# A hybrid gMLP / SSD block on one core: scan steps metered by engine weights, residual tiles fetched one tile ahead, last norms moved behind the first feed-forward unit

## The chip, the cores and the metric

The kernel runs on 1 of the 8 cores of one Trainium2 chip. The metric is the device time of one execution in microseconds. Everything below is read from the kernel's code, from the order of its built program, from three timed runs and from one profiled execution.

## What is computed

One layer of a hybrid backbone over 2048 latent tokens of width 1024, and 256 context tokens that only supply starting states. All matrices are float32.

```python
hl  = rms(x) * norm1_w * (1 + sc1) + sh1
proj = hl @ w_in                      # u, v (gMLP), z, x/B/C, dt
xbc = silu(conv5(xbc) + b)            # centred depthwise convolution
y   = ssd(forward) + flip(ssd(flipped))      # 16 heads, chunks of 128, states of 128 x 64
g   = (y + xs * d_skip) * silu(z);  ssd_out = rms(g, per group) * ssd_norm_w
gm_out = gelu(u) * (W_s @ rms(gelu(v)) * gm_norm_w + gm_bs)
x   = x + g1 * (concat(gm_out, ssd_out) @ w_out)
hl  = rms(x) * norm2_w * (1 + sc2) + sh2
x   = x + g2 * ((silu(hl @ w1) * (hl @ w3)) @ w2)
out = rms(x) * final_norm_w
```

## The kernel before

Every large product is made of three TensorE products of a high and a low part (`mm3`, lines 220 to 232): one output tile of 128 x 512 takes 24 matmuls of 512 columns, summed in one PSUM bank (tag `mmp`, four banks; the small products use four banks of tag `smp`). ScalarE makes the high part of each weight unit and VectorE the low part (line 217).

The tokens go in two blocks of 1024, and block 1 is projected first. The change concerns the long stretch that begins when block 0 projects z. Its main line is a chain of generators, one `yield` for each output tile of 24 matmuls: 16 tiles of `proj_z`, 16 of `proj_v`, 16 of `proj_u`, then `out_half` three times, 16 tiles each: block 1 with the gMLP half of w_out, block 0 with the gMLP half, block 0 with the SSD half. In the text these stages are z, v, u, oA, oB, oC. `early` loads the inputs of the next stage some tiles ahead (`load_mix`). The fourth `out_half` (block 1, SSD half; oD) comes after it, beside `border`, which prepares the first feed-forward unit. Then follow `ffn1(0)`, `ffn2(0)`, `ffn1(1)`, `ffn2(1)`; the feed-forward products use a seven-product scheme, whose moving operands `hl` 1 to 7 are made from the normed x (`prep_hl`, lines 997 to 1038) and in part parked in DRAM (`cscr`) and fetched back (`hl_back`, line 1044).

Beside the main line runs the side line: the last eight chunks of the backward state scan (`ssd_bwd`, 16 steps), then `ssd_y` for 16 chunks and two groups. One iteration of `ssd_y` (a chunk and a group) has two `y_seg` steps, which build the masked decay matrices out of 128 x 128 pieces (lines 722 to 733: two DMAs that spread a row of `fscr`, ScalarE line 728, VectorE line 729, ScalarE line 730, VectorE line 731, four times each, an exponential, a product on POOL), and `y_out` in three parts: the products with the two states and the diagonal product (lines 750 to 757), the state update and the sums (761 to 767), the gate with z read back from `zscr` (770 to 772). A chunk is normed by `y_norm` (a Newton square root of 11 small VectorE instructions, then line 780 on ScalarE), and `y_store` transposes it on TensorE (line 787) and stores it (line 790). The records of a chunk (`rec_sb`) lie in two buffers, the working tiles `tma` in 14.

`run` (line 876) sets the order: after each main step it takes `SIDE` = 2.74 side steps, whatever main or side step it is. The built program keeps an order near that one on each engine.

In `out_half` a tile's residual (x, or the x written by the half before) is loaded by line 849 after the tile's matmuls are issued, line 850 on VectorE adds the scaled product, and line 851 stores the sum. All of these transfers, the weights and the scan's loads among them, are issued in order by one queue, SP. In the second half the squares of the sums are gathered (`sq_acc`), and `rstd_store` (line 263) turns them into the reciprocal root of the next norm: a matmul with ones, a logarithm and an exponential on ScalarE, three VectorE steps, a store to `r2scr`. For block 1 the first 512 tokens' is made inside oD, the second's in the first unit of `ffn1(0)`.

Of the kernel before, what the change touches and what calls it, by code (L numbers as in the profile page):

```python
# [14 lines left out]
P = 128  # L15
# [14 lines left out]
NT2B = 3  # L30
# [7 lines left out]
SIDE = 2.74  # L38
# [44 lines left out]
def kernel(ctx: ExitStack, tc: tile.TileContext, xT, ctxp, cc, crow, wad1, wad2, vecs, rows,  # L83
# [506 lines left out]
    def proj_u(blk, hs):  # L590
        for h0 in range(0, 8, 2):
            us = [unit(U_U + h0), unit(U_U + h0 + 1)]
            for j in range(2):
                ts_ = slice((blk * 2 + j) * TB, (blk * 2 + j + 1) * TB)
                for i, (hi, lo) in enumerate(us):
                    m = tmp()
                    DMA.dma_start(m[:, :TB], mscr[h0 + i][:, ts_])
                    ps = mmp()
                    mm3(ps, [(hi[:, k * P:(k + 1) * P], lo[:, k * P:(k + 1) * P], hs[j][k][:, 0, :], hs[j][k][:, 1, :]) for k in range(KT)])
                    t = gelu2(ps, tmp)  # L600
                    V.tensor_tensor(out=t[:, :TB], in0=t[:, :TB], in1=m[:, :TB], op=ALU.mult)
                    DMA.dma_start(gmscr[h0 + i][:, ts_], t[:, :TB])
                    yield

    def proj_v(blk, hs):
# [17 lines left out]
        for hh in range(2):  # L623
            us = [unit(U_V + hh * 4 + i) for i in range(4)]
            for j in range(2):
                vh = []
                for c in range(4):
# [14 lines left out]
                    yield  # L642
                prev = (hh, j, vh)
        mixing(*prev)
        yield

    def proj_z(blk, hs):
        for g in range(2):
            us = [unit(U_Z + g * 4 + i) for i in range(4)]
            for c in range(8):  # L650
# [6 lines left out]
                yield  # L657
# [42 lines left out]
    def ssd_bwd(rp, hp, chunks):  # L700
        for c in chunks:
            for g in range(2):
                DMA.dma_start(hscr[c][:, g * TB:(g + 1) * TB], hst[(1, g)])
                if c > 0:
                    rc = load_rec(rp, c, g, False)
                    hst[(1, g)] = state_step(hp, rc, g, c, 1, hst[(1, g)])
                yield
# [7 lines left out]
    def y_seg(st, c, g):  # L715
        rc = st["rc"]
        Gt = []
        for q in range(2):
# [16 lines left out]
            yield  # L735
# [8 lines left out]
        yield  # L744

    def y_out(st, c, g, ms):
# [11 lines left out]
        yield  # L758
# [9 lines left out]
        yield  # L768
# [4 lines left out]
        yield  # L773
        return ya

    def y_norm(ys, ms):
# [4 lines left out]
        yield  # L781

    def y_store(ys, c):
        for g in range(2):
# [7 lines left out]
            yield  # L792
# [44 lines left out]
    def out_half(blk, half, hs, tmp=tma, last=None, last_acc=None):  # L837
        acc = [None, None]
        pend = None
        for m0 in range(0, 8, 2):  # L840
            us = [unit(U_O + half * 8 + m0), unit(U_O + half * 8 + m0 + 1)]
            for j in range(2):
                ts_ = slice((blk * 2 + j) * TB, (blk * 2 + j + 1) * TB)
                for i, (hi, lo) in enumerate(us):
# [3 lines left out]
                    t = tmp()  # L848
                    DMA.dma_start(t[:, :TB], xT[m * P:(m + 1) * P, ts_] if half == 0 else x2scr[m][:, ts_])
# [5 lines left out]
                    if half == 1:  # L855
                        acc[j] = sq_acc(acc[j], t[:, :TB], last_acc if last_acc and j == 1 and m == 0 else tmp)
# [8 lines left out]
                    yield  # L865

    def early(gen, total, lead, fn, box):
        for i in range(total):
            if i == total - lead:
                box.extend(fn())  # L870
            if next(gen, 0) is StopIteration:
                break
            yield
        yield from gen
# [70 lines left out]
    for _ in xbc(0, hs, None, dt_block(0, stat(hs))):  # L945
        pass
    m1, m0, s0, s1, h2 = [], [], [], [], []
    run((chain(proj_z(0, hs), proj_v(0, hs), early(proj_u(0, hs), 16, 6, lambda: [load_mix(2, 0), load_mix(3, 0)], m1),
               early(out_half(1, 0, m1), 16, 4, lambda: [load_mix(0, 0), load_mix(1, 0)], m0),
               early(out_half(0, 0, m0), 16, 4, lambda: [load_mix(0, 1), load_mix(1, 1)], s0),  # L950
               early(out_half(0, 1, s0), 16, 2, lambda: [load_mix(2, 1), load_mix(3, 1)], s1)), 1),
        (chain(ssd_bwd(rp, hp, range(7, -1, -1)), ssd_y(rp)), SIDE))


# [5 lines left out]
    accp = ctx.enter_context(tc.tile_pool(name="accp", bufs=1, reuse_waits="tile"))  # L960
# [148 lines left out]
    def ffn1(blk, raws, first=None):  # L1109
# [45 lines left out]
        for t in range(NJ + 1):  # L1155
# [10 lines left out]
            if blk == 0 and t == 0:  # L1166
                rstd_store(*box.pop())
# [200 lines left out]
```

## Time and profile before

| | us |
|---|---|
| median of 3 runs | 3001.41 (2999.85 to 3001.45) |
| the profiled execution, its own time | 3001.86 |
| its span | 2999.7 |
| PE busy | 2827.3 (94%) |
| weight loads busy | 2253.5 (75%) |
| VectorE (DVE) busy | 2002.9 (67%) |
| ScalarE (ACT) busy | 1295.7 (43%) |
| GpSimd (POOL) busy | 633.1 (21%) |

2.2 us of the execution lie outside the span. The busy time of PE is that of matmuls whose ends are modelled. Where PE has been idle for some microseconds, the granted clock falls to half for a while, which shows in the matmuls that follow: a busy PE is then a slower one. A number in brackets behind a row is the idle time of the engine before it, and what ended it.

### The profile page before, as it was taken

Reading aid. Unit: us, or ns where it says so; the run is one execution under the profiler, and the core shown is the slowest. Engines: PE = TensorE matmul, PEld = TensorE weight load, DVE = VectorE, ACT = ScalarE, POOL = GpSimd, SP = SyncE. Lnnn points to the kernel's source line nnn. Section 1 sums busy time; section 2 is a strip of 40 time slices with the busy share of each in tenths; the row PEclk is TensorE's granted clock in tenths of the full one; section 3 lists DMA queues with packets and bytes.
Section 4 is the critical chain, followed back from the end, with each engine's and each line's share of the span. In section 5 each row is a group of like instructions: output and inputs, shape, how many; then the busy total and the mean of one; then the engine's idle time right before and its main releaser. Section 6 shows DMA issues by size and latency. Waiting matters only on the chain. (4 is left out here: it accounts for less than half of the span.)

```text
span 2999.7 us, 37193 instructions
## 1 busy us (share of the span) xinstructions
PE 2827.3 (94%) x12474; PEld 2253.5 (75%) x12474; DVE 2002.9 (67%) x3412; ACT 1295.7 (43%) x2387; POOL 633.1 (21%) x550
## 2 busy tenths in 40 slices
PE   7999999999998988999888799999999899999997
PEld 2788778878676767777767588888778788888885
DVE  6777966886788889778764555555776544445555
ACT  4444343344355556445452533333554333333443
POOL 3100000210131223222202244444110322221000
PEclk8999999999999999999999899999999999999998
DMA  5222567732754668877756544445766433224664
GB/s 222 88 91 88 186 217 231 261 120 82 231 168 148 194 203 254 242 244 235 210 163 221 172 158 159 160 158 165 256 224 206 142 106 106 96 100 131 226 193 157
DMA packets 295531, 525.94 MB, mean 175 GB/s; under 512 B 28838, under 2 KB 89638, under 8 KB 295340
## 3 DMA queue, kind: packets, MB, share of 16 engines
q1 hardware_dynamic: 295340, 523.57, 54.4%
q8 instruction: 98, 1.61, 0.2%
q14 instruction: 93, 0.76, 0.1%
HBM read 380.84 MB, written 142.62 MB: 175 GB/s over the span
## 5 line engine op out<-in xcount | busy, mean ns | idle before, releaser
L979 DVE TENSOR_TENSOR hl<-w,hl 128x1024 fp32r<-128x1024 f32 x286 | 371.9, 1306 | 308.9 <-ACT hl L978 127.1
L978 ACT CAST hl<-w 128x1024 fp32r<-128x1024 f32 x286 | 298.3, 1049 | 427.4 <-PE mmp L1094 121.5
L230 PE MATMUL mmp<-actt,whi 128*128 128x512 f32 x1120 | 458.2, 409 | 14.4 <-DVE t L850 8.0
L231 PE MATMUL mmp<-actt,whi 128*128 128x512 f32 x1120 | 448.5, 400 | 0.0
L232 PE MATMUL mmp<-actt,wlo 128*128 128x512 f32 x1120 | 445.8, 398 | 0.0
L1093 PE MATMUL mmp<-hl,hl 128*128 128x512 f32 x704 | 276.2, 392 | 5.5 <-DVE t L1201 2.3
L1095 PE MATMUL mmp<-hl,hl 128*128 128x512 f32 x704 | 276.0, 392 | 0.5 <-DVE hl L979 0.5
L1094 PE MATMUL mmp<-hl,hl 128*128 128x512 f32 x704 | 275.8, 392 | 0.0
L230 PEld LDWEIGHTS mmp<-actt,whi 128*128 128x128 f32 x1120 | 216.4, 193 | 65.9 <-DVE t L850 10.5
L231 PEld LDWEIGHTS mmp<-actt,whi 128*128 128x128 f32 x1120 | 216.4, 193 | 48.5 <-issue 5.5
L232 PEld LDWEIGHTS mmp<-actt,wlo 128*128 128x128 f32 x1120 | 215.6, 193 | 47.8 <-issue 1.7
L1093 PE MATMUL smp<-hl,hl 128*128 128x512 f32 x528 | 210.1, 398 | 16.5 <-ACT hl L978 16.5
L230 PE MATMUL mmp<-whi,actt 128*128 128x512 f32 x512 | 211.8, 414 | 0.0
L1094 PE MATMUL smp<-hl,hl 128*128 128x512 f32 x528 | 208.9, 396 | 0.0
L1095 PE MATMUL smp<-hl,hl 128*128 128x512 f32 x528 | 207.4, 393 | 0.0
L232 PE MATMUL mmp<-whi,actt 128*128 128x512 f32 x512 | 207.2, 405 | 0.0
L231 PE MATMUL mmp<-wlo,actt 128*128 128x512 f32 x512 | 205.8, 402 | 0.0
L985 DVE TENSOR_TENSOR t<-smp,t 128x512 f32<-128x512 f32 x88 | 60.5, 688 | 187.8 <-PE smp L1095 146.5
L1093 PEld LDWEIGHTS mmp<-hl,hl 128*128 128x128 f32 x704 | 132.4, 188 | 36.1 <-issue 2.7
L452 DVE SCALAR_TENSOR_TENSOR tma<-xin,cw,tma 128x512 f32<-128x512 f32 x192 | 144.3, 751 | 21.5 <-ACT tma L450 15.9
L985 POOL TENSOR_TENSOR w<-w 128x512 f32<-128x512 f32 x44 | 58.6, 1333 | 458.5 <-DVE hl L979 316.9
L733 POOL TENSOR_TENSOR tma<-tma 128x512 f32<-128x512 f32 x64 | 87.4, 1366 | 318.9 <-ACT tma L732 222.4
(267 smaller groups left out, 5875.7 us busy)
## 6 DMA issues: line engine op xcount, KB each, us to landing
w<-in_wall_dram SPq DMA_DIRECT2D x110, 512.0 KB, 4.1
ws<-in_wall_dram SPq DMA_DIRECT2D x104, 512.0 KB, 4.4
ascr<-t SPq DMA_DIRECT2D x154, 256.0 KB, 4.0
w<-ascr SPq DMA_DIRECT2D x154, 256.0 KB, 2.8
tma<-fscr SPq DMA_DIRECT2D x128, 256.0 KB, 5.8
w<-wscr SPq DMA_DIRECT2D x88, 256.0 KB, 3.5
t<-x2scr SPq DMA_DIRECT2D x74, 256.0 KB, 4.6
w<-in_wall_dram SPq DMA_DIRECT2D x66, 256.0 KB, 3.6
```

The lines of the kernel that those rows point to most:

```text
L230: PE.matmul(ps, lhsT=lh, rhs=rh, start=(i == 0), stop=False)
L231: PE.matmul(ps, lhsT=lh, rhs=rl, start=False, stop=False)
L232: PE.matmul(ps, lhsT=ll, rhs=rh, start=False, stop=(i == n - 1))
L452: V.scalar_tensor_tensor(out=acc[:, :n], in0=raw[:, j:j + n], scalar=cw[:, ch, j:j + 1], in1=acc[:, :n], op0=ALU.mult, op1=ALU.add)
L733: G.tensor_tensor(out=A, in0=A, in1=fb, op=ALU.mult)
L978: S.copy(hi, x)
L979: eng.tensor_tensor(out=lo, in0=x, in1=hi.bitcast(F32), op=ALU.subtract)
L985: eng.tensor_tensor(out=o, in0=a, in1=b, op=ALU.add)
L1093: PE.matmul(ps, lhsT=hi[:, ms_], rhs=t[:, 0, :], start=first and k == 0, stop=False, skip_group_check=not first)
L1094: PE.matmul(ps, lhsT=hi[:, ms_], rhs=t[:, 1, :], start=False, stop=False, skip_group_check=not first)
L1095: PE.matmul(ps, lhsT=lo[:, ms_], rhs=t[:, 0, :], start=False, stop=k == 3, skip_group_check=not first)
```

## The change

Three edits.

The meter. `run` with `SIDE` gives way to `paced`. Each main and side step now yields a pair of weights, TensorE and VectorE microseconds (`W_MM` with `W_Z`, `W_V`, `W_U`, `W_O` for a main tile, `W_MIX` for the loading of a stage's inputs, and `W_ST` to `W_TR` for the side steps). After a main step, side steps are taken while the VectorE sum is below `SHARE` = 1.15 times the TensorE sum. A side step that needs a gate tile not yet written waits for it (`zdone`), and a stage that reads the stored scan makes sure it is there (`need`, `stored`).

The residual. `out_half` loads the residual of the next tile ahead of the sum of this one (`fetch`).

The norms. Both of block 1's `rstd_store` are made after the second round (t = 1) of the first feed-forward unit. For that a second buffer of the sum of squares is needed, and the pool `t2b` shrinks from three tiles to two: one more of the x tiles of `ffn2` is taken from the 14 tiles of `t2`.

```diff
-NT2B = 3
+NT2B = 2
-SIDE = 2.74
+SHARE = 1.15
+W_MM = 5.4
+W_Z, W_V, W_U, W_O, W_MIX = 1.4, 5.8, 2.8, 1.45, 11.4
+W_ST, W_SEG, W_Y1, W_Y2, W_Y3, W_NORM, W_TR = (0.85, 2.1), (0, 3.2), (2.9, 1.4), (0.85, 3.0), (0, 0.7), (0, 3.7), (1.0, 0)
...
@@ y_out
-        yield
+        yield W_Y2
+        while zdone[0] < min(g * 8 + c + 1, g * 8 + 8):
+            yield None
         zt = tma()[:, :TB]
...
@@ out_half
+        def fetch(m, j):
+            t = tmp()
+            ts_ = slice((blk * 2 + j) * TB, (blk * 2 + j + 1) * TB)
+            DMA.dma_start(t[:, :TB], xT[m * P:(m + 1) * P, ts_] if half == 0 else x2scr[m][:, ts_])
+            nxt.append(t)
+        todo = [(m0 + i, j) for m0 in range(0, 8, 2) for j in range(2) for i in range(2)]
+        fetch(*todo.pop(0))
...
-                    t = tmp()
-                    DMA.dma_start(t[:, :TB], xT[m * P:(m + 1) * P, ts_] if half == 0 else x2scr[m][:, ts_])
+                    t = nxt.pop(0)
+                    if todo:
+                        fetch(*todo.pop(0))
...
                             pend = (acc[j], r2scr[blk * 2 + j], tmp)
-                            if j == 1:
-                                if last is None:
-                                    rstd_store(*pend)
-                                else:
-                                    last.append(pend)
+                            if last is not None:
+                                last.append(pend)
                                 pend = None
-                    yield
+                            elif j == 1:
+                                rstd_store(*pend)
+                                pend = None
+                    yield W_MM, W_O
-    def early(gen, total, lead, fn, box):
-        for i in range(total):
+    def early(gen, total, lead, fn, box, need=0):
+        for i, w in enumerate(gen):
             if i == total - lead:
+                yield need
                 box.extend(fn())
-            if next(gen, 0) is StopIteration:
-                break
-            yield
-        yield from gen
+                yield (0, W_MIX)
+            yield w
+    def paced(main, side, share):
+        pe = dve = 0.0
+        for w in main:
+            if isinstance(w, int):
+                while stored[0] < w:
+                    next(side)
+                continue
+            pe, dve = pe + w[0], dve + w[1]
+            while dve < share * pe:
+                w = next(side, None)
+                if w is None:
+                    break
+                pe, dve = pe + w[0], dve + w[1]
+        for _ in side:
+            pass
...
@@ ffn1
-            if blk == 0 and t == 0:
-                rstd_store(*box.pop())
+            if box and t == 1:
+                for b in box:
+                    rstd_store(*b)
+                box.clear()
```

What the meter does to VectorE's queue in stage v is seen here, at two of the 16 tiles. Before (575 and 577 are the gelu of a v tile, 635 to 243 its square root, 637 its scaling, 729 and 731 the scan's 128 x 128 steps, 757 and 763 the scan's outputs):

```order
L637 TENSOR_TENSOR xin<-xin,sml 128x512
L731 SCALAR_TENSOR_TENSOR tma<-rec_sb,dt_sb,tma 128x128 x4
L577 SCALAR_TENSOR_TENSOR xin<-xin,mmp 128x512
L777 TENSOR_SCALAR sml<-sml 128x2
L217 TENSOR_TENSOR wlo<-ws,whi 128x1024
L729 SCALAR_TENSOR_TENSOR tma<-tma,acs 128x128 x4
L757 TENSOR_TENSOR tma<-smp,eac 128x512
L635 TENSOR_SCALAR sml<-sml 128x4
L575 SCALAR_TENSOR_TENSOR xin<-xin,mmp 128x512
L238 TENSOR_SCALAR sml<-sml 128x4
L763 TENSOR_TENSOR h_2515<-h_2515,smp 128x512
```

Now (lines are 3 higher up to line 640):

```order
L580 SCALAR_TENSOR_TENSOR xin<-xin,mmp 128x512
L640 TENSOR_TENSOR xin<-xin,sml 128x512
L220 TENSOR_TENSOR wlo<-ws,whi 128x1024
L638 TENSOR_SCALAR sml<-sml 128x4
L241 TENSOR_SCALAR sml<-sml 128x4
L242 TENSOR_SCALAR sml<-sml 128x4
L244 TENSOR_TENSOR sml<-sml 128x4
L578 SCALAR_TENSOR_TENSOR xin<-xin,mmp 128x512
L245 SCALAR_TENSOR_TENSOR sml<-sml 128x4
```

Most of the scan's rows have left stage v. Counted by the matmul of line 751 in TensorE's order, the iterations that stand in z, v, u, oA, oB, oC were 3, 5, 7, 6, 6, 5 and are 5, 2, 5, 9, 8, 3; the chunks transposed in oA, oB, oC were 4, 3, 3 and are 4, 4, 3.

SP's queue at the end of oD, before (849 loads a residual, 851 stores a sum, 1044 fetches `hl` 6 and 5 back, 267 stores a norm):

```order
L849 DMA t2_14390<-x2scr7_168 128x512
L1199 DMA x2t_17959<-x2scr0_161 128x512
L851 DMA x2scr7_168<-t2_14390 128x512
L1044 DMA t2_14401<-cscr6_0_191 128x512
L849 DMA t2_14434<-x2scr6_167 128x512
L1054 DMA w4_14608<-in_wall_dram 128x1024
L851 DMA x2scr6_167<-t2_14434 128x512
L849 DMA t2_14476<-x2scr7_168 128x512
L267 DMA r2scr2_159<-t2_14440 1x512
L851 DMA x2scr7_168<-t2_14476 128x512
L1044 DMA t2_14522<-cscr5_0_195 128x512
```

Now (856 loads, 873 stores, 1080 fetches back):

```order
L856 DMA t2_14356<-x2scr7_168 128x512
L873 DMA x2scr6_167<-t2_14318 128x512
L856 DMA t2_14392<-x2scr6_167 128x512
L873 DMA x2scr7_168<-t2_14356 128x512
L1080 DMA t2_14403<-cscr6_0_191 128x512
L856 DMA t2_14436<-x2scr7_168 128x512
L873 DMA x2scr6_167<-t2_14392 128x512
L1237 DMA x2t_17959<-x2scr0_161 128x512
L873 DMA x2scr7_168<-t2_14436 128x512
L1080 DMA t2_14512<-cscr5_0_195 128x512
```

Each residual's load now stands ahead of the store of the tile before it; it stood behind. The norm's store is gone from here.

ScalarE's queue where the first of block 1's norms is made, before (between the casts of `hl` 6, line 978, at the end of oD; 248 and 249 are the logarithm and the exponential):

```order
L978 CAST hl_0_14495<-t_14401 128x512
L248 ACT_TABLE_LOAD
L248 ACTIVATE t_14440<-smp,eps_t 128x512
L978 CAST hl_1_14496<-t_14403 128x512
L249 ACT_TABLE_LOAD
L249 ACTIVATE t_14440<-t_14440 128x512
L978 CAST hl_2_14497<-t_14405 128x512
```

Now (1169 is a silu of the first unit, 251 and 252 the same two functions, 1014 the cast):

```order
L1169 ACTIVATE t_14804<-t_14804 128x512
L251 ACT_TABLE_LOAD
L251 ACTIVATE t_14822<-smp,eps_t 128x512
L252 ACT_TABLE_LOAD
L252 ACTIVATE t_14822<-t_14822 128x512
L1014 CAST hl_14717<-t_14706 128x512
```

Four instructions that stood between the casts of the border stand behind a silu of the first unit.

## Rows read from the trace of the kernel before

**Rows 1.** Busy time by stage: z, v, u, oA, oB, oC, oD, border.
```profile
core 0: us, PE busy (x) PEld busy (x) DVE busy (x) ACT busy (x) POOL busy (x), PEclk, DMA share, GB/s
735.40:860.20 124.80, 120.81 (x509) 89.72 (x509) 89.48 (x174) 50.99 (x120) 22.16 (x18) 0.99 0.60 193
860.20:1006.10 145.90, 127.79 (x591) 101.87 (x590) 128.33 (x379) 86.47 (x278) 33.32 (x28) 0.94 0.47 145
1006.10:1149.80 143.70, 132.06 (x610) 101.86 (x609) 117.98 (x277) 79.11 (x196) 41.12 (x31) 0.96 0.72 228
1149.80:1287.20 137.40, 124.81 (x549) 97.88 (x548) 113.50 (x242) 71.31 (x171) 38.60 (x31) 0.94 0.81 244
1287.20:1416.00 128.80, 121.36 (x538) 94.81 (x537) 96.51 (x210) 61.85 (x151) 35.58 (x30) 0.96 0.76 231
1416.00:1549.40 133.40, 117.97 (x522) 92.92 (x521) 93.21 (x190) 64.00 (x138) 21.19 (x19) 0.94 0.65 200
1549.40:1656.70 107.30, 96.80 (x388) 76.25 (x386) 51.77 (x75) 38.43 (x56) 17.05 (x11) 0.94 0.62 201
1656.70:1697.40 40.70, 20.10 (x65) 13.14 (x64) 29.11 (x37) 24.18 (x35) 7.47 (x5) 0.75 0.68 232
```

**Rows 2.** Whom PE waited for, 735.4 to 1549.4: total, times, longest.
```profile
PE smp L787 <- ACT tma L780: 34.5, 9, 8.4
PE smp L615 <- DVE xin L637: 6.0, 2, 4.6
```

**Rows 3.** Whom VectorE waited for, the same stretch.
```profile
DVE tma L729 <- ACT tma L728: 56.7, 38, 4.4
...
DVE tma L850 <- DMA tma<-in_xT_dram: 11.7, 5, 4.2
...
DVE tma L850 <- DMA tma<-x2scr: 10.8, 7, 6.2
```

**Rows 4.** Timeline of PE in oC, with its longest wait.
```profile
1506.19 1.12 PE L787 MATMUL smp<-ident,tma 128*128 128x128 f32 x4 [8.45 <-ACT tma L780]
...
1507.53 0.63 PE L231 MATMUL mmp<-actt,whi 128*128 128x512 f32 x1
...
1512.85 0.39 PE L230 MATMUL mmp<-actt,whi 128*128 128x512 f32 x1
...
1515.35 1.02 PE L750 MATMUL smp<-h,rec_sb 128*128 128x512 f32 x2
...
1518.77 0.48 PE L230 MATMUL mmp<-actt,whi 128*128 128x512 f32 x1
```

**Rows 5.** Timeline of the queue SP shortly before that wait.
```profile
1478.59 0.53 SPq L849 DMA_DIRECT2D tma<-x2scr  x1
1489.10 0.32 SPq L851 DMA_DIRECT2D x2scr<-tma  x1
```

**Rows 6.** Whom the queue SP waited for, oA to oC.
```profile
SPq L851 <- DVE tma L850: 64.5, 33, 5.6
SPq L851 <- DMA tma<-x2scr: 34.3, 10, 7.2
SPq L687 <- POOL tma L766: 27.7, 11, 3.4
```

**Rows 7.** Whom PE and VectorE waited for, oD and border.
```profile
PE mmp L230 <- DVE t L850: 8.0, 6, 3.0
...
DVE t L850 <- DMA t<-x2scr: 26.2, 9, 4.4
```

**Rows 8.** Timelines of ACT, SP and PE in the border.
```profile
1666.37 1.28 ACT L248 ACT_TABLE_LOAD   x1
...
1674.77 0.42 SPq L849 DMA_DIRECT2D t<-x2scr  x1
...
1679.52 9.87 SPq L1044 DMA_DIRECT2D t<-cscr  x16
...
1683.11 0.79 PE L1093 MATMUL smp<-hl,hl 128*128 128x512 f32 x1 [16.53 <-ACT hl L978]
```

**Rows 9.** Whom PE waited for in the first `ffn2`, 2090 to 2400.
```profile
PE mmp L1221 <- DVE hl L979: 4.5, 2, 2.4
```

More of the change, by code (lines that the diff above doesn't have):

```diff
@@ L641, in proj_v @@
                         mixing(*prev)
-                    yield
+                    yield W_MM, W_V
                 prev = (hh, j, vh)
         mixing(*prev)
-        yield
+        yield 0, 0
+    zdone = [0]
     def proj_z(blk, hs):
@@ L656, in proj_z @@
                 DMA.dma_start(zscr[blk * 8 + c][:, g * TB:(g + 1) * TB], t[:, :TB])
-                yield
+                zdone[0] += 1 - blk
+                yield W_MM, W_Z
     def state_in(rc, g, ci, d):
@@ L734, in y_seg @@
             Gt.append(A)
-            yield
+            yield W_SEG
         st["G"] = Gt
@@ L743, in y_seg @@
         st["hb"] = hb
-        yield
+        yield 0, 0
     def y_out(st, c, g, ms):
@@ L772, in y_out @@
         S.activation(zt, ya, AF.Square, accum_out=ms[:, g:g + 1])
-        yield
+        yield W_Y3
         return ya
@@ L780, in y_norm @@
             S.activation(ys[g], ys[g], AF.Copy, scale=r[:, g:g + 1])
-        yield
+        yield W_NORM
     def y_store(ys, c):
@@ L791, in y_store @@
                           t.rearrange("p (i t) -> p i t", t=P))
-            yield
+            yield W_TR
+        stored[0] = c + 1
+    stored = [0]
     def ssd_y(rp):
@@ L855, in out_half @@
                     if half == 1:
[L856 removed]
+                        acc[j] = sq_acc(acc[j], t[:, :TB], last_acc if last_acc and m == 0 else tmp)
                         if m == 7:
                             pend = (acc[j], r2scr[blk * 2 + j], tmp)
[L859 to L868 removed]
+                            if last is not None:
+                                last.append(pend)
+                                pend = None
+                            elif j == 1:
[4 more added lines that the diff above has]
+        for i, w in enumerate(gen):
             if i == total - lead:
+                yield need
                 box.extend(fn())
[L871 to L874 removed]
+                yield (0, W_MIX)
[15 more added lines that the diff above has]
+            pass
     def run(*gens):
@@ L947 @@
     m1, m0, s0, s1, h2 = [], [], [], [], []
[L948 to L952, printed above, removed]
+    paced(chain(proj_z(0, hs), proj_v(0, hs), early(proj_u(0, hs), 16, 6, lambda: [load_mix(2, 0), load_mix(3, 0)], m1),
+                early(out_half(1, 0, m1), 16, 4, lambda: [load_mix(0, 0), load_mix(1, 0)], m0),
+                early(out_half(0, 0, m0), 16, 4, lambda: [load_mix(0, 1), load_mix(1, 1)], s0, 8),
+                early(out_half(0, 1, s0), 16, 2, lambda: [load_mix(2, 1), load_mix(3, 1)], s1, 16)),
+          chain(ssd_bwd(rp, hp, range(7, -1, -1)), ssd_y(rp)), SHARE)
     mix.close()
@@ L959 @@
     late = []
-    accp = ctx.enter_context(tc.tile_pool(name="accp", bufs=1, reuse_waits="tile"))
+    accp = ctx.enter_context(tc.tile_pool(name="accp", bufs=2, reuse_waits="tile"))
     def acc1():
```

7 lines of the change are left out of this document (4 added, 3 removed).

## The prediction

> **What bounds the kernel now.** I first read the page's summary: PE is busy for 94% of the span and no other engine for over 67%, so time can only come from PE's idle stretches and from matmuls at the lower clock. The busy time by stage [rows 1] says where these are. The reader is to see three columns: the length of a stage less PE's busy time, which is PE's idle time; PEclk; and VectorE's busy time. PE idles for 4.0, 18.1, 11.6, 12.6, 7.4 and 15.4 us in z, v, u, oA, oB and oC (69.1 in all), 10.5 in oD and 20.6 in the border. These 962 us hold all the places that the change touches, but for one round of `ffn1` and the pool of `ffn2`.
>
> The idle time costs more than itself. After the wait of 8.45 us the matmuls take 0.63 us a piece instead of 0.39 for some 5 us [rows 4]; that is the lower of the clock's two levels, 1.2 instead of 2.4 GHz. The missing clock times the length gives 1.2, 8.8, 5.7, 8.2, 5.2 and 8.0 us for z to oC, 37 in all: 0.54 us for each us of idle time. I therefore price an idle us in these stages at 1.54 us.
>
> Then I asked what ends the waits. Half of the idle time, 34.5 us, is PE at a transposition of the scan's output, waiting for ScalarE's line 780, that is for the norm of a chunk [rows 2]; 6.0 more is the mixing of v, waiting for VectorE. In v VectorE is busy for 128.3 of 145.9 us, 88%, the highest share of any stage [rows 1]: there it has too much to do. In oA to oC it has room (83, 75 and 70%) and still comes late. VectorE waits 56.7 us for ScalarE's line 728, which waits for transfers, and 22.5 us for the residual (11.7 and 10.8) [rows 3]. Before the longest wait the queue SP issues a residual's load at 1478.59 and then nothing until 1489.10, when the store of that tile can go [rows 5]: whatever the scan needs from memory stands behind that store. From oA to oC SP stands 64.5 us before such stores for VectorE's line 850, and 34.3 us more by way of the residual's load [rows 6].
>
> **The change part by part.** *The meter.* It adds and removes no instruction, it moves the scan. Without idle time and slow clock the stages take 119.6, 119.0, 126.4, 116.6, 116.2 and 110.0 us (length less idle less missing clock), 708 in all, and that sum stays. An iteration is 3.42 us of PE from the products with the states to the next projection matmul [rows 4], and about 0.9 for the state update, a product of the shape of line 750's, which takes 1.02 with its tail: 4.3 us. With the iterations counted in the built program (+2, -3, -2, +3, +2, -2) the stages come to 128.2, 106.1, 117.8, 129.5, 124.8 and 101.4.
>
> How much PE will idle beside them is not in the trace, so I bound it by stages. oB idles 7.4 us for 6 iterations, 1.2 each; oA 2.1; oC 3.1; z, where nothing crowds, 1.3. I take 1.3 for all 32, near oB, because the change takes away what sets oA and oC apart: VectorE's wait for the residual there. With 2 us left for the mixing in v this makes 43.6 us of idle time instead of 69.1, and at 1.54 a saving of 39 us. The ends: 0.8 each saves 64 us; oA's 2.1 for all leaves nothing. Against it stands VectorE in oA: its rows between oA's matmuls in the built program, each at the mean time of its line, add up to 120 us before and 141 now, so its busy time there rises from 113.5 to some 134; at the 88% of stage v it needs 152 us, where the sum above gives 147.5. I add 4.5 us. **The meter: -35 us** (-64 to +5).
>
> The new waits of the side line for a gate tile cost nothing in this sum: by the weights one step waits, near the end of the first half of z, and the scan catches up beside the next tile. If SP stood there until that tile's store has landed, two or three transfers would be late by one tile, 5 us at most; that is within the range.
>
> The trace of before also has a reason why the meter should not help. SP waits 27.7 us for POOL's line 766, which frees one of the two record buffers [rows 6], and the change gives no buffer. The Trainium skill, in Perfetto Trace Analysis under Optimization Strategy, says that a gap repeating through a stretch can mean too little SBUF or PSUM for the next tile. By that rule the nine waits for line 780 would stay and the meter's term would be 0 instead of -35. The row bears it out in part, since 27.7 is less than half of the 64.5 us that SP stands for stores, so the rule is a rival below and not the forecast.
>
> *The residual in oD.* PE waits 8.0 us in six places for line 850, and VectorE 26.2 us for the residual [rows 7]. Loaded a tile ahead, 107.3 / 16 = 6.7 us earlier, the residual is there: VectorE's longest wait for it is 4.4 us. 8.0 us at 1.54 is 12; I take **-10 us** (-14 to -4), as `border`'s own loads, on which VectorE also waits, stay in the same queue. The extra tile lies in the same pools; where it makes a load wait for a buffer, the loss is the same kind of SP wait and is in the ends.
>
> *The end of oD and the border.* The last two sums wait for each other: load at 1674.77, and only after the last store do the 16 loads of parked operands begin, at 1679.52, 23 us after the last projection matmul (oD ends at 1656.7); PE starts again at 1683.11 after 16.53 us [rows 8]. In between ScalarE makes a norm, with a table load at 1666.37, and VectorE stands behind it. With both residuals loaded early and the norm gone, the last store should go some 2 us after the last matmul and the loads by 1660. From the first load to PE's start it took 3.6 us, so the operands are there at about 1663 to 1665; PE has 24 matmuls that need none of them, as many as a tile of oD, (107.3 - 10.5 - 6.4) / 16 = 5.6 us, to 1663. So I leave 2 us of the 16.5, and give back 1.5 us of slow matmuls after it: **-16 us** (-19 to -8). Late next are VectorE's splits of the parked operands, 16 of them in a row, hence not the whole wait.
>
> *The norms in the first unit.* The same instructions, two table loads each, now together in round 1. PE waits there little and its matmuls are queued ahead: **+1 us** (0 to 4). Their readers come a whole `ffn1` later.
>
> *The tile less in `ffn2`.* PE waits 4.5 us there for VectorE's splits [rows 9], beside the preparation of block 1, which shares the 14 tiles. One tile less can make SP wait for a buffer while later loads stand behind: **+2 us** (0 to 8).
>
> The sum is -35 - 10 - 16 + 1 + 2 = -58. The profiled execution took 3001.9 us (2999.7 of span and 2.2 around it), 0.4 above the median of the runs. 3001.9 - 58 = **2944 us**.
>
> **The rivals.** *The gaps stay.* The waits before the transpositions come from the buffers and from ScalarE's waits for transfers, not from crowding; the meter shifts them and the sum of z to oC stays at 814 us. For it: the 56.7 and 27.7 us above, and oC, which idles most with VectorE at 70%. Against it: v and u. Only -10 - 16 + 3 = -23 is left: 2979 us.
>
> *Slower: every chunk stalls as the worst one does.* oA and oB now take 9 and 8 iterations instead of 6 and 6, and 11 chunks are transposed in oA to oC instead of 10. If VectorE, with no room left there, brings each norm as late as the one at 1506 [rows 4], a chunk costs 8.45 us and 11 matmuls at 0.2 us more, 10.7 together. 11 of them are 118 us, against 56.8 us of idle time and missing clock now: +61. z, v and u still save 25 and the rest 23: +13, 3015 us. It decides from 9.5 us a chunk, (56.8 + 48) / 11. Against it: oB loses 12.6 us in three chunks, 4.2 each, and the residual's wait goes.
>
> *The change doesn't do what it says.* If the scheduler or the pools held the loads back, the residual would still come late. In the built order the loads do stand ahead, so I give this no chance of its own; it is in the lower half of the second case.
>
> **How the numbers follow.** The forecast 0.60, with 2915 to 2972 by the ends above; the gaps stay 0.25, 2965 to 2995; slower 0.10, 3008 to 3030; something else 0.05. The range takes most of the first two: 2912 to 2988. A measurement of this kernel can tell about 0.2%, 6 us, from no change. Faster by more than that: 0.60 and nearly all of the 0.25, 0.84. Within it 0.06, slower 0.10.
>
> **What would show it.** Right: PE's idle time from z to oC falls from 69 to about 44 us and PEclk in v rises from 0.94 to 0.97; v takes some 30 us less, oA some 15 more; VectorE's rows of waiting for `t<-x2scr` and `tma<-x2scr` at the sums are gone; the wait of 16.5 us before the first unit is under 4. Wrong: waits for line 780's successor sum to 34 us or more; or oA and oB together take over 310 us; or the first `ffn2` has new waits of over 8 us.

## The result, and the profile after

The changed kernel takes 3018.70 us (median of 4 runs, 3015.06 to 3020.35) against 3000.63 (4 runs, 2996.12 to 3001.45) for the kernel before: 1.0062 times, 95% interval 1.0044 to 1.0079. The forecast was 2944, with 2912 to 2988 as its range. The sign is wrong, and the time is near that of the slower rival (3015).

Busy time by stage in the changed kernel, in the order of [rows 1] (z, v, u, oA, oB, oC, oD, border); columns as there:

```profile
738.60:888.70 150.10, 135.14 (x552) 97.13 (x551) 112.07 (x226) 62.52 (x156) 32.13 (x27) 0.96 0.58 184
888.70:1015.60 126.90, 115.77 (x540) 93.66 (x541) 101.28 (x317) 71.01 (x231) 17.74 (x14) 0.96 0.43 134
1015.60:1148.20 132.60, 120.44 (x544) 95.14 (x543) 107.07 (x229) 66.86 (x158) 30.26 (x24) 0.95 0.71 217
1148.20:1304.20 156.00, 137.05 (x616) 106.05 (x614) 130.24 (x281) 83.22 (x206) 49.66 (x42) 0.93 0.77 230
1304.20:1464.50 160.30, 135.47 (x593) 104.60 (x592) 128.60 (x281) 82.19 (x206) 53.64 (x41) 0.90 0.77 231
1464.50:1581.60 117.10, 107.33 (x474) 85.82 (x473) 74.27 (x137) 53.74 (x101) 12.01 (x9) 0.94 0.65 206
1581.60:1671.10 89.50, 88.32 (x387) 72.21 (x385) 56.45 (x77) 35.75 (x53) 16.57 (x11) 1.00 0.69 227
1671.10:1711.80 40.70, 24.16 (x87) 18.51 (x87) 28.35 (x35) 22.74 (x36) 12.03 (x9) 0.79 0.63 218
```

The reader is to see length less PE busy, PE's idle time. It grew where the meter put work: 15.0 us in z, 18.9 in oA and 24.8 in oB, against 4.0, 12.6 and 7.4 before. Where the meter took work away it fell in v (11.1 against 18.1) and oC (9.8 against 15.4), but not in u (12.2 against 11.6); from z to oC it is 91.8 against 69.1. The missing clock grew with it, 51.6 against 37. Whom PE waited for from z to oC (total, times, longest), to be held against [rows 2]:

```profile
PE smp L795 <- ACT tma L788: 36.4, 7, 10.9
PE smp L795 <- DVE tma L762: 18.3, 3, 7.3
PE mmp L233 <- DVE tma L660: 6.4, 2, 4.3
PE smp L795 <- ACT tma L738: 5.9, 1, 5.9
```

Line 795 is the transposition (787 before), 788 ScalarE's copy with the norm (780 before), 762 VectorE's reading of a bank of `smp`. With a row of 2.9 us, waits at the transposition come to 63.5 us; before, all rows of line 787 together came to 45. Whom VectorE waited for at the residual's sum in the same stretch, to be held against [rows 3]:

```profile
DVE tma L872 <- PE mmp L235: 36.5, 14, 4.8
DVE tma L872 <- DMA tma<-in_xT_dram: 0.8, 1, 0.8
```

The waits for the residual's load, 22.5 us before, are down to 0.8; VectorE now waits at the sum for PE.

The whole difference of the two spans, 3016.7 - 2999.7 = 17.0 us, is split here (us; forecast in the third column, from the terms of the prediction; oC's end before is taken 0.2 us later than in [rows 1]):

| stretch | before | forecast | after |
|---|---|---|---|
| up to z | 735.4 | 735.4 | 738.6 |
| z to oC | 814.2 | 779 | 843.0 |
| oD | 107.1 | 97 | 89.5 |
| end of oD to the first matmul of `ffn2` | 451.3 | 436 | 450.8 |
| from there to the end | 891.7 | 894 | 894.8 |

In the border the wait of 16.5 us [rows 8] has split. Timelines of PE, VectorE and POOL there (start, length, engine, line, then the idle time before it and its cause):

```profile
1679.84 0.79 PE L1131 MATMUL mmp<-hl,hl 128*128 128x512 f32 x1 [4.44 <-DVE hl L1015]
...
1699.05 0.80 PE L1131 MATMUL mmp<-hl,hl 128*128 128x512 f32 x1 [9.03 <-DVE hl L1015]
...
1677.90 0.75 DVE L872 SCALAR_TENSOR_TENSOR t<-mmp,m_sb,t 128x512 f32<-128x512 f32 x1 [3.97 <-DMA t<-x2scr]
...
1681.47 4.91 DVE L1015 TENSOR_TENSOR hl<-t,hl 128x512 fp32r<-128x512 f32 x8
...
1687.43 10.43 DVE L1015 TENSOR_TENSOR hl<-t,hl 128x512 fp32r<-128x512 f32 x10
...
1687.66 1.60 POOL L1021 TENSOR_TENSOR w<-w 128x512 f32<-128x512 f32 x1 [14.96 <-DVE hl L1015]
1689.35 3.28 POOL L1018 TENSOR_TENSOR w<-w,w 128x512 f32<-128x512 f32 x2
1692.59 1.72 POOL L1018 TENSOR_TENSOR t<-w,w 128x512 f32<-128x512 f32 x1
```

The last residual is still late by 3.97 us, and PE then stands twice for VectorE's splits of the operands (line 1015). Eight of them take 4.91 us; ten take 10.43, as four of the ten take 1.75 to 1.78 us beside POOL and the others 0.68.

### The profile page after: what moved, and what is told of

Its sections match the earlier page's. It is cut to its first block, busy times and chain, and to the rows that moved or that the text cites. A ratio compares the mean times of both kernels' runs of the same rounds, so it can differ in the third digit from the quotient of the medians.

```text
span 3016.7 us, 37234 instructions
## 1 busy us (share of the span) xinstructions
PE 2825.4 (94%) x12474; PEld 2255.4 (75%) x12474; DVE 2023.4 (67%) x3412; ACT 1298.1 (43%) x2388; POOL 640.0 (21%) x550
## 5 line engine op out<-in xcount | busy, mean ns | idle before, releaser
L1131 PEld LDWEIGHTS mmp<-hl,hl 128*128 128x128 f32 x704 | 133.7, 190 | 43.0 <-DVE hl L1015 14.3
L1129 PEld LDWEIGHTS mmp<-hl,hl 128*128 128x128 f32 x704 | 133.8, 190 | 39.7 <-ACT t L1154 4.0
L219 ACT CAST whi<-ws 128x1024 fp32r<-128x1024 f32 x104 | 108.5, 1045 | 117.7 <-PE mmp L234 66.6
```

The costliest lines, as they stand in the source:

```text
L1129: PE.matmul(ps, lhsT=hi[:, ms_], rhs=t[:, 0, :], start=first and k == 0, stop=False, skip_group_check=not first)
L1131: PE.matmul(ps, lhsT=lo[:, ms_], rhs=t[:, 0, :], start=False, stop=k == 3, skip_group_check=not first)
```

## The experiments

The ratios are against the kernel before on the same chip. The stages come from one profiled execution of each kernel, on several chips, and such an execution can lie well off the median of its runs: e13's 7.0, e16's 6.3 and e17's 5.6 us over, e9's 5.8 and e14's 4.6 under. A difference of stages under some 10 us is therefore no more than a hint where the ratios don't bear it out. "Held" is worked out from the trace: for every VectorE row from z to oC that takes over 1.3 times the lower quartile of its line and shape, what it takes over that quartile, summed.

| run | ratio, 95% interval | z to oC | held | oD | oD end to `ffn2` |
|---|---|---|---|---|---|
| before | 1 | 814.2 | 69 | 107.1 | 451.3 |
| changed kernel | 1.0062, 1.0044 to 1.0079 | 843.0 | 76 | 89.5 | 450.8 |
| e1 residual alone | 0.9951, 0.9936 to 0.9966 | 809.8 | 72 | 101.1 | 438.2 |
| e2 meter alone | 1.0090, 1.0074 to 1.0105 | 839.6 | 68 | 102.3 | 451.0 |
| e3 no meter | 0.9964, 0.9951 to 0.9978 | 807.4 | 70 | 95.0 | 451.6 |
| e16 no norms' move | 1.0058, 1.0040 to 1.0075 | 842.0 | 76 | 96.5 | 440.1 |
| e4 late transpositions | 1.0060, 1.0043 to 1.0076 | 834.2 | 78 | 89.4 | 451.3 |
| e11 transpositions on `mmp` | 1.0138, 1.0125 to 1.0151 | 859.0 | 77 | 89.4 | 451.4 |
| e12 both | 1.0120, 1.0105 to 1.0136 | 851.9 | 79 | 89.7 | 450.7 |
| e6 e1, late transpositions | 0.9952, 0.9940 to 0.9965 | 819.0 | 61 | 96.7 | 438.6 |
| e10 three record buffers | 1.0069, 1.0056 to 1.0083 | 834.3 | 83 | 89.5 | 450.8 |
| e7 no gate | 1.0090, 1.0074 to 1.0105 | 841.3 | 77 | 89.5 | 450.2 |
| e5 `SHARE` 1.08 | 1.0017, 1.0009 to 1.0026 | 815.0 | 72 | 93.4 | 453.0 |
| e8 no decay | 0.9927, 0.9913 to 0.9940 | 798.4 | 36 | 89.5 | 452.0 |
| e9 decay on VectorE | 1.0003, 0.9994 to 1.0012 | 812.7 | 36 | 89.5 | 451.8 |
| e14 xd on VectorE | 1.0027, 1.0014 to 1.0039 | 820.9 | 61 | 89.5 | 451.0 |
| e13 e1, decay on VectorE | 0.9919, 0.9900 to 0.9939 | 804.5 | 34 | 100.2 | 440.3 |
| e15 1.08, decay on VectorE | 0.9957, 0.9940 to 0.9974 | 790.9 | 39 | 112.7 | 443.7 |
| e17 1.12, decay on VectorE | 0.9972, 0.9962 to 0.9983 | 812.7 | 38 | 97.7 | 438.7 |
| e18 e13, xd on VectorE | 0.9924, 0.9910 to 0.9937 | 805.0 | 20 | 101.2 | 438.5 |

**The parts.** e1 is the kernel before with the hunks of `fetch`; e2 the changed kernel without them and without the norms' hunks; e3 the changed kernel with `run` and `SIDE` = 2.74; e16 the changed kernel with `NT2B = 3`, `accp` of one buffer and the old `rstd_store` calls.

> The kernel before with one part of the change alone: each residual tile is fetched one tile ahead. Theory A (the meter is what costs): oD is 15 to 20 us shorter, as in the changed kernel (107.1 to 89.5), z to oC stay at 814 us within 6, the border stays (the norm and late loads are still there, at most 5 us less): 2980 to 2987 us. Rival (the early fetch costs in z to oC, because a tile more is held and SP stands for a buffer): oD is shorter all the same, but oA to oC, 397 us before, grow by 10 to 30, and the time is 2990 to 3010 us.

> The changed kernel with the meter alone: residual loads where they were before, norms where they were before. Theory A (the meter costs): z to oC take about 843 us, as in the changed kernel, oA and oB together over 305, waits at the transpositions of the scan's output 55 to 75 us; oD 107 and the border as before: 3025 to 3040 us. Rival (the early fetch costs, not the meter): z to oC take 815 us or less and the time is at or under that of the kernel before, 2985 to 3000 us.

> The changed kernel without the meter: one scan step beside so many projection tiles as before, but residuals a tile ahead and the last norms in the first unit. Theory A: 2975 to 2987 us, z to oC near 814 us, oD near 90, and the stretch from the end of oD to the first matmul of the second feed-forward product unchanged (451 us within 4), because VectorE's and ScalarE's splits, not the norm, end the wait there. Rival (the border gains as forecast, and only the meter's state of VectorE at its end hid it): the 16.5 us wait before the first unit falls under 5 us and the time is 2960 to 2970 us.

> The changed kernel with the last norms where they were (meter and residual stay). If the norms' move costs, as the two runs without a meter say (the stretch from the end of oD to the second product of the first unit 451.6 us with the move and 438.2 without, oD 95.0 and 101.1): this stretch falls from 450.8 to 438 to 445, oD grows from 89.5 to 93 to 101, and the time is 2 to 8 us under the changed kernel's. If the move gains under the meter, as forecast (16 us): the time is 8 to 16 us over it.

The meter alone costs 0.9%, the residual alone gains 0.5%: theory A. In e1 and e2 it missed in oD, which the residual alone shortens by 6.0 us, not 15 to 20. e1's gain is in the border as well as in oD, against at most 5 us expected there: the loads of the parked operands begin at 1646.75, 2.1 us after the last projection matmul, with the norm still there, and the wait of 16.5 us is 9.1. The norms' move only shifts time: oD is 7 us shorter (96.5 to 89.5 under the meter, 101.1 to 95.0 without it) and the stretch behind it 11 to 13 longer. In time e16 stands 0.0004 under the changed kernel (2 to 8 us forecast) and e3 0.0013 over e1, both inside the intervals: no gain, and a loss that isn't settled.

**The order of the transpositions.** e4 `if store is not None and g == 0:` → `g == 1:`; e11 `ps = smp()` → `ps = mmp()` in `y_store`; e12 both; e6 is e1 with e4's line.

> The changed kernel with one line altered: the transpositions of a chunk's output stand half a chunk later in the order (beside the second half of the next chunk instead of its first). Theory T1 (the meter sets PE's transposition too close behind the norm that it waits for; only the order is wrong): the waits at the transpositions, 63.5 us in the changed kernel, fall under 20 us, z to oC take 780 to 815 us and the time is 2960 to 2995 us. Theory T2 (VectorE cannot do more in z, oA and oB, whatever waits for it): the transposition waits fall too, but PE waits instead at the projections' accumulators, at the products of the scan or at the mixing for VectorE; z to oC stay over 830 us and the time is 3005 to 3025 us.

> The changed kernel with the transpositions writing to a bank of mmp (the projections' four accumulators) instead of smp (the scan's four). Theory S (part of the waits at the transposition is a wait for a bank of smp that VectorE has yet to read, 18.3 us by the rows that name lines 762 and 763): these rows go, the waits of 36.4 us for ScalarE's copies stay, z to oC fall by 8 to 25 us. If VectorE's lateness, not the bank, is what PE waits for: the waits move to the products of the scan or to ScalarE's copy, and z to oC stay within 8 us of 843.

> Both: transpositions half a chunk later and on banks of mmp. With late transpositions alone the waits for ScalarE's copies went and waits for a bank of smp came in their place (39.5 us for line 763). Theory S with T1: neither is left, waits at the transpositions are under 15 us instead of 63.5, z to oC take 775 to 808 us and the time is 25 to 60 us under the changed kernel's. Otherwise PE meets the same late VectorE at the next product of the scan: z to oC stay over 822 us.

> The kernel before with residual tiles a tile ahead and with the transpositions half a chunk later; no meter, norms where they were. By T2 VectorE has room in oA to oC of the old order (83, 75 and 70% busy), so a later transposition is a wait less: z to oC fall from 810 us in the run without late transpositions to 780 to 797, and the time is 10 to 28 us under that run's 2977. By the rival (VectorE's lateness goes on to the next instruction of PE that needs it, a product of the scan or a buffer of smp, there as in the metered order, where late transpositions gave back 9 us): z to oC 800 to 810 us, time 2968 to 2978.

Whom PE waited for from z to oC in e4, the first rows:

```profile
PE smp L795 <- DVE tma L763: 39.5, 6, 8.7
PE smp L795 <- ACT tma L738: 10.4, 2, 5.8
...
PE smp L795 <- ACT tma L788: 1.8, 3, 1.0
```

in e11 the first row:

```profile
PE mmp L795 <- ACT tma L788: 58.3, 13, 9.9
```

and in e12:

```profile
PE mmp L795 <- ACT tma L788: 15.9, 3, 8.6
PE smp L756 <- DVE tma L762: 13.5, 4, 6.3
PE mmp L233 <- DVE tma L872: 13.5, 5, 8.1
```

Late transpositions nearly end the wait for the norm (1.8 us) and meet VectorE's reading of a bank. With another bank alone the waits for a bank of `smp` go from the transposition, but the wait for the norm rises from 36.4 to 58.3 us; z to oC grow by 16, which neither case of e11 has. With both, PE meets the norm (15.9), VectorE at the next product (756) and the projections' own accumulators (233 for 872). T1 and theory S fall, and e4 lies within T2's numbers: wherever the transposition stands, something of VectorE's is late. The old order gains nothing either: e6 stands 0.0001 from e1, and its z to oC, 819.0 us, lie outside both cases (z starts 7.2 us earlier there than in e1).

**The record buffers.** e10: `NREC = 3`, `NTMA = 13`.

> The changed kernel with three record buffers instead of two, paid for with one tile less of tma (13 instead of 14). Theory B (the scan's turn is held by its two record buffers: SP stands 81.8 us from z to oC for POOL's last reading of a record, and all later loads behind it): that wait falls under 20 us, z to oC fall by 20 to 45 us from 843, the time by 20 to 50. If SP stands there with time to spare: z to oC stay within 8 us, the wait of SP moves to the stores, and the time stays within 8 us of the changed kernel's.

SP's wait for POOL's line 772 fell from 81.8 to 59.3 us only, so the theory's first number failed; the time did not move, though the tile of `tma` that pays for the buffer may have a price of its own. Of the prediction's rule of the Trainium skill (Perfetto Trace Analysis, Optimization Strategy: a repeating gap can mean too little SBUF or PSUM), this run shows that a third record buffer at that price doesn't help; no run has more of both.

**VectorE's work, and how crowded it is.** e7 drops `V.tensor_tensor(out=ya, in0=ya, in1=zt, op=ALU.mult)`; e5 sets `SHARE = 1.08`.

> The changed kernel without VectorE's product of the scan's output with the gate tile (ya times zt, 32 instructions of 0.69 us, 17 of them in oA and oB); the load and ScalarE's square stay. Its output lacks the gate. T2 (VectorE is late in oA and oB): oA and oB together fall by 11 to 22 us from 316, z to oC by 15 to 32 from 843, the time by 12 to 32. If PE's stalls come from the order or from a wait for memory alone: oA and oB fall by less than 5 us and the time by less than 8.

> The changed kernel with one number altered: SHARE 1.08 instead of 1.15, so that the scan is spread to the end of oC (it ends beside tile 12 of oC instead of tile 2; oA and oB have 7 iterations each instead of 9 and 8). Theory T2 (VectorE, given more weight than TensorE, is what comes late in oA and oB): oA and oB together fall from 316 us to 280 to 298, oC grows from 117 to 128 to 145, z to oC take 815 to 832 us and the time is 10 to 28 us under the changed kernel's. Theory T1 (every chunk stalls at its transposition because of the order, whatever VectorE has to do): the stalls move to oC with the chunks, z to oC stay at 838 us or more and the time is within 6 us of the changed kernel's.

e7 refuses T2 as stated: 22 us less of VectorE's work gained nothing (1.0090 against 1.0062, 841.3 us from z to oC). e5 fits it in time (0.0045 under the changed kernel, 13 us), z to oC are at the end of its range, and it misses in where the time lies: oA and oB take 138.2 and 129.9 us with 7 iterations each, and oC 168.2 with 8 (forecast at most 145).

```profile
1115.70:1253.90 138.20, 127.18 (x570) 99.32 (x569) 114.25 (x256) 75.80 (x184) 50.66 (x35) 0.95 0.79 245
1253.90:1383.80 129.90, 123.26 (x566) 96.28 (x565) 102.57 (x224) 68.60 (x171) 42.55 (x35) 0.99 0.75 235
1383.80:1552.00 168.20, 130.83 (x590) 102.00 (x589) 135.94 (x288) 83.58 (x198) 44.78 (x34) 0.89 0.66 203
```

So idle time goes with crowding from oA to oC: with 7 iterations PE idles 11.0 and 6.6 us; with 8 it idles 37.4 in oC here and 24.8 in oB above. The count alone doesn't decide: z has 5 in both orders and idles 5.5 us here, 15.0 in the changed kernel. What holds VectorE in a crowded stage these runs don't say.

**POOL's hold.** VectorE's and POOL's timelines in oB of the changed kernel, ahead of PE's longest wait (10.94 us, to 1356.96):

```profile
1344.95 3.74 DVE L737 SCALAR_TENSOR_TENSOR tma<-rec_sb,dt_sb,tma 128x128 f32<-128x128 f32 x4
1348.62 1.12 DVE L735 SCALAR_TENSOR_TENSOR tma<-tma,acs 128x128 f32<-128x128 f32 x4
...
1344.32 1.87 POOL L739 TENSOR_TENSOR tma<-tma 128x512 f32<-128x512 f32 x1 [5.63 <-DMA tma<-fscr]
1346.14 1.09 POOL L745 TENSOR_TENSOR tma<-rec_sb,ddt 128x512 f32<-128x512 f32 x1
1347.20 1.08 POOL L768 TENSOR_TENSOR h<-h,tot 128x512 f32<-128x512 f32 x1
...
1356.18 1.33 ACT L788 ACTIVATE tma<-tma,sml 128x512 f32<-128x512 f32 x2 [5.73 <-DVE sml L246]
```

Four rows of 128 x 128 take 3.74 us while POOL's three products run, and the next four 1.12 behind them. The norm that ScalarE waits for (`sml` of line 246) lies in the same queue. In oA and oB the held time is 42.6 us, against 25.4 before. Over the whole stretch it hardly differs, though (76 and 69, and 68 in e2, the meter alone): the hold is a cost of both orders, and the meter gathers it in two stages. e8 drops POOL's `G.tensor_tensor(out=A, in0=A, in1=fb, op=ALU.mult)`; e9 makes it `V.tensor_tensor`; e14 does so with `xd` instead.

> The changed kernel without POOL's product with the decay (A times fb, two instructions an iteration, 64 in all, of some 1.2 us on POOL); ScalarE's exponential stays. Its output lacks the decay. Theory P (POOL's instructions hold up VectorE's between SBUF tiles: in the changed kernel's trace VectorE's rows take 0.35 us alone and 1.0 to 1.2 us where POOL runs through them, together 42 us in oA and oB): with 2 of 5 of POOL's instructions gone 12 to 20 of the 42 us go, oA and oB fall by 12 to 25 us and the time by 15 to 40. If POOL only waits its turn and costs VectorE nothing that PE feels: only PE's waits for that product go (3.3 us), and the time falls by less than 8 us.

> The changed kernel with the product with the decay (A times fb) on VectorE instead of POOL: 64 instructions leave POOL, VectorE gets 64 of 0.69 us, 44 us. Theory P (POOL's instructions hold up VectorE's and lengthen the scan's chain; VectorE's own work is not what PE waits for, since 22 us less of it moved nothing): most of what leaving the product out gave (40 us) is kept, the time is 12 to 40 us under the changed kernel's. If VectorE's busy time sets the stages: the time is 15 to 45 us over the changed kernel's.

> The changed kernel with another of POOL's products moved to VectorE: the weighted inputs (xd, 30 instructions of 1.14 us on POOL, 0.69 on VectorE), which nothing waits for soon; the decay's product stays on POOL. Hold theory (any POOL instruction holds up VectorE, on average 76 / 156 = 0.5 us each): some 15 us less of stretched rows, z to oC fall by 3 to 15 us, the time by 3 to 15. Chain theory (the decay's product mattered because PE's products and the next iteration wait for it): no gain, the time 0 to 15 us over the changed kernel's, as VectorE has 21 us more.

In time all three fit theory P (0.0135, 0.0059 and 0.0035 under the changed kernel: 40, 18 and 10 us). z to oC lost 44.6, 30.3 and 22.1 us (3 to 15 forecast for e14) against the changed kernel, with 41, 40 and 16 us less held, though e9 gives VectorE 44 us more to do and e14 some 21. A product nobody waits for soon (xd) pays too, so the decay's place in the chain is not the reason alone, and the hold fits all three. It isn't shown by itself: each run also gives POOL less to do, and none takes the hold away and leaves POOL's work where it is. Whom PE waited for in e9, z to oC, and e9's row of oB:

```profile
PE smp L757 <- DMA tma<-hscr: 17.6, 10, 7.9
PE smp L795 <- ACT tma L788: 15.9, 10, 3.5
...
1269.70:1429.30 159.60, 135.50 (x604) 102.36 (x604) 131.89 (x302) 84.12 (x210) 32.52 (x26) 0.96 0.76 234
```

With a longest wait of 3.5 us for the norm, the clock's share falls as well: 19.9 us are missing instead of 51.6. But a new wait came, at line 757 for loads of the stored backward states (`hscr`; 17.6 us, 1.8 in the changed kernel), and oB, the longest stage, is as long as before, 159.6 us with 24.1 of idle time (160.3 and 24.8), though its held time fell from 21.2 to 11.8 us.

**Both together, and the old order.** e13 is e1 with e9's line, e18 adds e14's; e15 and e17 are the changed kernel with e9's line, e16's hunks and `SHARE` 1.08 and 1.12.

> The old order (no meter, norms where they were) with residual tiles a tile ahead and the decay's product on VectorE: the run of the residual alone, 0.9951 of the kernel before, plus one moved product. If POOL's hold on VectorE costs in the old order as in the metered one (VectorE's rows are stretched by 72 us from z to oC there, 76 in the changed kernel): 10 to 25 us under that run, 2952 to 2968 us, ratio 0.986 to 0.992. If only the crowded stages of the meter felt it: within 6 us of that run, or slower by up to 15, since VectorE gets 44 us and is 88% busy in v.

> The meter at 1.08, residual a tile ahead, the decay's product on VectorE, the last norms where they were before the change. If crowding (8 and 9 iterations in a stage) and POOL's hold are separate causes, both gains add up: 13 us from the share and 18 from the product under the changed kernel's 1.0062, ratio 0.991 to 0.998. If they are one (a less crowded VectorE is held up less): no more than the product alone gave, ratio 0.998 to 1.003.

> The meter at 1.12 with the decay's product on VectorE, residual a tile ahead, norms where they were before the change. At 1.08 this saved 14 us from z to oC against the old order with the same other parts (790.9 and 804.5) and lost 12.5 in oD (112.7 and 100.2), where PE waited 4.6 us for the scan's last chunk. If it is the late end of the scan that costs oD: at 1.12 it ends five tiles of oC earlier, oD takes 96 to 104 us, z to oC 790 to 803, ratio 0.990 to 0.994. If crowding sets in again from 1.12: oA or oB over 150 us, ratio 0.995 to 1.000.

> The fastest run so far (old order, residual a tile ahead, decay's product on VectorE, 0.9919 of the kernel before) with xd on VectorE as well. Hold theory: another 5 to 12 us, ratio 0.988 to 0.991. If the old order has VectorE full in v and u, where it now gets 21 us more: 0.992 to 0.997.

In e15 the two gains add up, as its first case had it: 0.0105 under the changed kernel, against 0.0045 and 0.0059 for share and product alone. In z to oC it is the fastest of all runs, 790.9 us, 13.6 under the old order with the same parts (e13, whose profiled execution is 7.0 over its median), and oC with 8 iterations takes 142.7 instead of 168.2 in e5. oD gives 12.5 of it back, and in time e15 is 14.5 us slower than e13 on the same chip. The rows of oC and oD:

```profile
1385.60:1528.30 142.70, 130.87 (x589) 101.19 (x588) 123.29 (x279) 78.91 (x190) 25.53 (x20) 0.95 0.68 218
1528.30:1641.00 112.70, 99.00 (x399) 78.34 (x397) 64.40 (x96) 46.49 (x68) 15.56 (x11) 0.92 0.69 229
```

With the scan ending earlier (e17) oD is 97.7 again, but oA and oB have 8 iterations each, oB takes 159.3, and the gain is gone: its second case. In the old order the same product gains 0.0032 or 10 us between e1 and e13, whose intervals just overlap; ratio and time lie at the weak end of e13's first case, z to oC, 5.3 us less, do not. xd gains nothing more (e18, its second case): u has 22.3 us of idle time there instead of 15.8. e13, 2965.25 us against 2991.22, is the fastest, with e18 not to be told from it, and both beat the kernel before and the changed one.

## Why the prediction was wrong

**The meter, -35 forecast, +28.8 measured.** The step that failed is the idle time: "I take 1.3 for all 32, near oB, because the change takes away what sets oA and oC apart". The moved work was right. Length less idle less missing clock is 129.1, 110.7, 113.8, 126.2, 119.5 and 100.3 us, 699.6 in all, where the prediction put 128.2, 106.1, 117.8, 129.5, 124.8 and 101.4, 708. Idle time and missing clock came to 143.4 us instead of the 71.6 that 1.3 us an iteration, 2 for the mixing and 4.5 for VectorE's share in oA make at 1.54. Idle time alone is 91.8 us, where 43.6 were forecast: 8.5 us over in z, 6.5 in v, 5.7 in u, 7.2 in oA, 14.4 in oB and 5.9 in oC. An iteration's idle time is not a constant: before, 6 iterations cost 1.2 us each in oB and 2.1 in oA; now 8 cost 3.1 in oB and 9 cost 2.1 in oA, and in e5 7 cost 0.9 and 1.6, 8 cost 4.7. The low sample was taken at 6 in oB and used everywhere. Crowding is only part of it: 18.1 of the 48.2 us lie in v, u and oC, which lost iterations. The residual's wait did go from oA to oC, as foretold: VectorE waits 0.8 us for it there. In e1, with 7.0 us of it left, oC idles 9.9 us with 5 iterations, like oB (10.1 with 6), but oA 14.0 with 6: it wasn't what set oA apart.

VectorE's limit was priced in oA alone, 4.5 us, from its rows at their mean times in the old order. oA came out at 156.0, which that sum gives within 4 us (129.5 + 18 + 4.5 = 152); oB, with a VectorE nearly as busy (128.6 of 160.3), was left without it and is 19.5 us over its sum of 140.8, z and v 12 and 14 over theirs. The meter's weights have the same gap: rows at their time alone, and a share of 1.15 that hands VectorE more than TensorE, without what POOL holds and what VectorE waits for ScalarE.

Two of the prediction's signs of being wrong came: the waits for line 780's successor sum to 36.4 us (34 or more), and oA and oB take 316.3 (over 310). The range was also narrower than its own terms: the meter's end of +5 alone gives 2984 us, and the upper ends add up to 3007, where the forecast's own case stopped at 2972. **The gaps stay**, the 2979 us rival, had the waits for the norm right (34.5 and 36.4 us) but not their price: z to oC did not stay at 814.

**The slower rival** gave 3015 us from 10.7 us a chunk over 11 chunks. The total is near in part by luck: oA to oC grew by 34 us, not 61, while z to u saved 5, not 25, and the rest 12, not 23. PE waits 5.4 us a chunk at the transpositions over the 8 of oA and oB, not 8.45. That each norm itself takes longer is refused: from its first to its last VectorE row (785 to 246) a norm takes 10.1 us in the mean of 16 chunks, and 11.3 before.

**The residual, -10 forecast; -19 with the border.** Direction right, size short: e1's oD and the stretch behind it lose 6.0 and 13.1 us; in time e1 gains 0.0049, 15 us. The prediction had the second part in the border's term, with the norms.

**The border, -16 forecast, -0.5 measured.** The step "the loads by 1660", 3 us after oD's end, holds in e1 by the fetch alone (2.1 us) and fails in the changed kernel, where oD ends earlier and the last residual lands late: the 16 loads begin at 1679.05, 8.0 us after its end. "So I leave 2 us of the 16.5" failed: VectorE's splits, named there as late next, hold PE 9.0 and 4.4 us, and POOL adds 4.3 us to ten of them. **The norms** are followed by one new wait for ScalarE, 3.4 us in the changed kernel and 3.5 in e3, against 1 us forecast. **The tile less** shows no cost: the stretch to the end, +3.1 for +2 in this pair, takes 890.4 to 894.5 us in the nine kernels with three tiles and 890.3 to 896.0 in the eleven with two.

**What stays open.** That the meter's order costs is shown (e2, and e5 for its share); what in it costs is argued. Held time is no larger in e2 (68 us) than before (69). In time, 41, 40 and 16 us less of it gave 40, 18 and 10 us in the metered order, and 38 less gave 10 in the old one (e13 against e1), while 22 us less of VectorE's own work gave none; whether the metered order pays more for a microsecond of hold isn't settled. That the hold works through the norm isn't borne out either: its rows lie among other rows in VectorE's queue, but a norm takes 11.6 us in e9 and 10.1 in the changed kernel. A norm whose rows stand together wasn't tried. The 3.2 us before z have no cause here: that stretch takes 726.6 us (e6) to 743.5 (e17) in these runs.

## What to carry to other kernels

Idle time per piece of side work is no constant: here it was 1.2 to 2.1 us at one density and 0.9 to 4.7 at others, and stages that lost work waited longer than forecast too. A forecast that multiplies it has to be tried at two settings before it is believed (here `SHARE` 1.15 and 1.08, 13 us apart). A meter that adds up rows at their time alone misses the time that a second engine takes from the first. Taking that overlap away paid in both orders; that a meter then pays is not shown, since e15 is slower than e13. Where three repairs of one wait only move it to the next reader of the same engine, stop moving and ask what slows that engine.

## What the runs showed of the hardware

Many VectorE instructions with two tiles of SBUF as inputs are held by POOL's. From z to oC of the changed kernel line 737 takes 0.345 us alone (201 rows) and 0.907 in the mean where POOL runs through it (15 rows, 0.34 to 1.38: not each is held), the norm's line 244 0.159 and 0.990; in the border the splits take 0.68 us and, four times in a row beside POOL, 1.75 to 1.78. Rows that read one operand from PSUM are not held: line 771 takes 0.677 and 0.683 us, line 872 0.748 and 0.744. One input in SBUF does not spare a row by itself: the norm's line 242, which reads one tile, takes 0.165 us alone and 1.22 and 1.24 in the two rows that lie inside POOL's.

The Trainium skill (SBUF — State Buffer, Who interferes with whom) states that a VectorE instruction with two inputs in SBUF contends with a GpSimd instruction that reads SBUF, and that one with at most one such input doesn't, outside the modes that use both ports. The trace agrees on the first and on the rows with PSUM, with the numbers above; no run shows in which mode line 242 ran. What such a hold costs TensorE the runs had to show.
